# RWKV grams of a two-block transformer kernel: masked tiles of one kind each

## The chip, the cores and the metric

The kernel runs on one core of a Trainium2 chip. A core has a matrix engine (TensorE, PE in the profile; its weight loads are listed as PEld), three engines for elementwise work (VectorE or DVE, ScalarE or ACT, GpSimd or POOL), SyncE (SP), which here issues the weight transfers, and DMA queues. Each engine works through its own instructions in order and waits on semaphores for the others. The metric is the device time of one execution in microseconds (us), given as the median of several runs.

## The reference

The program takes 256 tokens of width 2048 in fp32 through two blocks. The first is a hybrid: one projection `u = rmsnorm(x) @ w_in` feeds an attention with forget gates ("fox", 8 heads of 128) and an RWKV7 recurrence (16 heads of 64), whose outputs are gated and merged. The second block joins a gated convolution, a latent attention and a memory attention. The change concerns the recurrence, which the reference writes step by step:

```python
def step(S, inp):
    r_t, w_t, k_t, v_t, kk_t, b_t = inp
    sa = jnp.einsum('bhvk,bhk->bhv', S, -kk_t)
    S = (S * w_t[:, :, None, :] + sa[..., None] * b_t[:, :, None, :]
         + v_t[..., None] * k_t[:, :, None, :])
    y = jnp.einsum('bhvk,bhk->bhv', S, r_t)
    return S, y
...
y = _rwkv7_scan(rh, heads(decay), kh, vh, kk, kk * ah)
mu = jnp.mean(y, axis=-1, keepdims=True)
var = jnp.mean(jnp.square(y - mu), axis=-1, keepdims=True)
y = ((y - mu) * lax.rsqrt(var + GN_EPS)).reshape(B, T, RWKV_WIDTH)
y = y * rwkv_ln_w.astype(f32) + rwkv_ln_b.astype(f32)
...
o_b = (y + bonus.reshape(B, T, RWKV_WIDTH)) * jax.nn.silu(z_b)
...
o_a = o_a.astype(x.dtype) @ w_proj_fox
o_b = o_b.astype(x.dtype) @ w_proj_rwkv
m = jax.nn.sigmoid(g_a) * o_a + jax.nn.sigmoid(g_b) * o_b
return x + m @ w_out
```

## The kernel before

**GEMMs.** All projections run as one stream of weight blocks of 512 KB. SyncE fetches a block into `raw` (L402), ScalarE rounds it to `whi` (helper at L278), VectorE takes `wlo = raw - whi` (helper at L241), and TensorE multiplies (L286) with activations split in the same way: three products (whi with the high part, whi with the low part, wlo with the high part), which together give fp32 precision. There are four `raw` and four `whi`/`wlo` buffers. A product is named by its GEMM: `acc.fq`, `acc.fk`, `acc.fv`, `acc.fz` (fox), `acc.zb` (the RWKV gate), `acc.ga` and `acc.gb` (the gates of the merge), `acc.pf` and `acc.pr` (the two output projections), and so on; `acc.gb` comes right after the last `acc.pf` column.

**Side work.** RWKV, fox heads and the like are generators ("jobs"). Between weight blocks a planner steps them: it keeps clocks of estimated costs for each engine and decides at each block which job goes one `yield` on. A scheduler then puts the resulting instructions in an order per engine and gives out the buffers. So the order of instructions on an engine depends on the costs of the steps and on when buffers come free. Two pools matter here: `a4` gives 32 slots of 128 x 1024 words in SBUF, and three PSUM banks serve the side work (grams, attention scores `fs`, transposes `fpt`, outputs `fo`), while five banks hold the GEMMs' sums. A tile that is handed out is sometimes claimed by a one-element memset on VectorE (L565): it stands in VectorE's order, and whoever writes the tile first waits for it.

**RWKV.** A job treats 8 heads, so it runs in two halves (about 115 to 375 us and 400 to 635 us). The 256 tokens are cut into four chunks `c` of 64, the heads into four pairs `j`; a unit `u = 4j + c` is one pair in one chunk, so there are 16. Per unit and head `hh` of the pair, TensorE forms the gram of `AR` and `BK`. Its left 64 columns (kind r = 0) are masked strictly and its right 64 columns (r = 1) inclusively by the constant `rmask` (128 columns). This is done in four rounds `q` of four units: eight matmuls into two PSUM banks (one per `hh`), a `yield`, two mask products on VectorE into the tile `GG`, four DMAs on GpSimd's queue that copy 32 x 32 corners of the strict part to DRAM (`Ld`, L954), a `yield`. The strict part is read three times: through `Ld` by the inversion of the triangular systems (tiles `W`, `LB`, `Xd`, `XA`), by the matmul `u` (L995 and around) and by `zl` (L1024). `zl` stands ahead of the loop over four chunks (L1031 on). The inclusive part is read in that loop by `yp` (L1073). Behind the loop come `CE` and `SQ` (centred outputs and squares), `head_rs` (mean squares `hs` by matmul, an inverse square root by integer steps and Newton steps on VectorE in the tiles `hms`, `ht`, `hg`, `hy`, then `hy` written to DRAM as `hd` and read back spread over partitions as `hr`, L622 to L627), then `CE *= hr`, `BV += CE`, `BV *= szb`, and the split of `BV` into `obh`, `obl`, which `acc.pr` multiplies.

**Fox.** For each head `fs` (scores) goes through softmax on VectorE and ScalarE (`sm`, `mx`), is transposed by TensorE (`fpt`, L1184), copied to `PT` on ScalarE and multiplied by the values (`fo`). These steps stand between the RWKV steps in zb, between 410 and 460 us.

**Merge.** `gate` is the sigmoid of `acc.ga` or `acc.gb` (ScalarE), `mf` is gate times `acc.pf` (VectorE). Both are `a4` tiles and are claimed.

Of the kernel before, what the change touches and what calls it, by code (L numbers as in the profile page):

```python
# [226 lines left out]
def hybrid_kernel(ctx: ExitStack, tc: tile.TileContext, io, out):  # L227
# [15 lines left out]
    def mul(o, a, b):  # L243
        tt(o, a, b, ALU.mult)
# [38 lines left out]
    def mm(o, l, r, start=True, stop=True):  # L283
        n = fsz(o)
        clock["pe"] += max(PEF + n / 2400.0, 0.109) if l.dtype == F32R else max(n / 600.0, fsz(l) / 1200.0)
        TE.matmul(o, lhsT=l, rhs=r, start=start, stop=stop)  # L286
# [17 lines left out]
    def a4(name, dt=F32):  # L304
        return apool.tile([128, 4, 256], dt, name=nm(name), tag="a4")
# [28 lines left out]
    def cc(n, p0=0, p1=128, c0=0, c1=None):  # L334
        o, w = CCOL[n]
        t, o = (con, o) if o < NCON2 else (con1, o - NCON2)
        return t[p0:p1, o + c0:o + (w if c1 is None else c1)]
# [391 lines left out]
    for b in range(4):  # L729
# [11 lines left out]
        for acc, cols, blocks in ((acc_l, 256, [b]), (acc_r, 512, [4 + 2 * b, 5 + 2 * b])):  # L741
            per = 1024 // cols
            for c, o in enumerate(acc):
                for e, j in enumerate(blocks):
                    for i in range(per):
                        k = per * e + i
                        w = slice(i * cols + 128 * c, i * cols + 128 * c + 128)
# [83 lines left out]
    def rwkv_job(b):  # L831
# [46 lines left out]
        for i in range(2):  # L878
            us = slice(8 * i, 8 * i + 8)
            for hh in range(2):  # L880
                p = slice(64 * hh, 64 * hh + 64)
# [8 lines left out]
        for i in range(2):  # L890
            us = slice(8 * i, 8 * i + 8)
            for hh in range(2):
                p = slice(64 * hh, 64 * hh + 64)
# [19 lines left out]
        SV = [a4("SV").rearrange("p a b -> p (a b)").rearrange("p (u k s) -> p u k s", u=8, k=2) for _ in range(2)]  # L913
        for i in range(2):
# [9 lines left out]
            ps3 = ps.rearrange("p (u s) -> p u s", u=8)  # L924
            for u in range(8):
                for hh in range(2):
                    p, q = slice(64 * hh, 64 * hh + 64), slice(64 - 64 * hh, 128 - 64 * hh)
# [4 lines left out]
            for hh in range(2):  # L932
                q = slice(64 - 64 * hh, 128 - 64 * hh)
                acopy(SV[i][q, :, hh, :], ps3[q, :, :])
            yield
        GG = []
        Ld = dpool.tile([2, 2, 16, 32, 32], F32, name=nm("Ld"), tag="Ld", bufs=2)
        for q in range(4):
            g = a4("GG").rearrange("p a b -> p (a b)").rearrange("p (u k r t) -> p u k r t", u=4, k=2, r=2)
            GG.append(g)  # L940
            pg = [bank("gram"), bank("gram")]
            for w in range(4):
                u = 4 * q + w
                for hh in range(2):
                    p = slice(64 * hh, 64 * hh + 64)
                    mm(pg[hh][:, 128 * w:128 * w + 128], BK[u // 8][p, u % 8, :, :], AR[u // 8][p, u % 8, :, :])
            yield
            for hh in range(2):
                mul(g[:, :, hh, :, :].rearrange("p u r t -> p u (r t)"), pg[hh].rearrange("p (u m) -> p u m", u=4),
                    cc("rmask").unsqueeze(1).to_broadcast([128, 4, 128]))  # L950
            for hh in range(2):
                for hf in range(2):
                    p0 = 64 * hh + 32 * hf
                    POOL.dma_start(out=Ld[hh, hf, 4 * q:4 * q + 4, :, :].rearrange("u s t -> s u t"),  # L954
                                   in_=g[p0:p0 + 32, :, hh, 0, 32 * hf:32 * hf + 32])
            yield
        W1, W2, W3 = a4("W1"), a4("W2"), a4("W3")
        LB = flat(W1)[0:64, :].rearrange("p (s t) -> p s t", s=32)
# [9 lines left out]
        for j in range(31):  # L968
            n, w = 31 - j, j + 1
# [11 lines left out]
        XA = b2("XA").rearrange("p (u c) -> p u c", u=16)  # L981
        for hh in range(2):
            POOL.dma_start(out=XA[64 * hh:64 * hh + 32, :, :], in_=Xd[hh, 0, :, :, :].rearrange("u t c -> t u c"))
            for hf in range(2):
                p0 = 64 * hh + 32 * hf
                POOL.dma_start(out=YF[p0:p0 + 32, :, 32 * hf:32 * hf + 32],
                               in_=Yd[hh, hf, :, :, :].rearrange("u s t -> s u t"))
# [4 lines left out]
        for u in range(16):  # L992
            for hh in range(2):
                p0 = 64 * hh
                mm(ps3[p0 + 32:p0 + 64, u, :], GG[u // 4][p0:p0 + 32, u % 4, hh, 0, 32:64], XA[p0:p0 + 32, u, :])  # L995
            if u == 7:
                yield
        yield
# [20 lines left out]
        for i in range(2):  # L1019
            zl = bank("zl").rearrange("p (u v) -> p u v", u=8)  # L1020
            for w in range(8):
                u = 8 * i + w
                for hh in range(2):
                    mm(zl[hs[hh], w, :], GG[u // 4][hs[1 - hh], u % 4, hh, 0, :], SV[i][hs[1 - hh], w, hh, :])  # L1024
                if w == 3:
                    yield
            yield
            acopy(ZL[:, 8 * i:8 * i + 8, :], zl)

        S = None  # L1030
        for c in range(4):  # L1031
            u_of = lambda j: 4 * j + c
            Z = ZL[:, c:16:4, :]
            yp = bank("yp")[:, :256].rearrange("p (j v) -> p j v", j=4)
            if S is not None:
                z = bank("z")[:, :256].rearrange("p (j v) -> p j v", j=4)
                for j in range(4):
                    u = u_of(j)
                    for hh in range(2):
                        mm(z[hs[hh], j, :], AR[u // 8][hs[hh], u % 8, 0, :], S[hs[hh], j, :])  # L1040

                for j in range(4):
                    u = u_of(j)
                    for hh in range(2):
                        mm(yp[hs[hh], j, :], S[hs[hh], j, :], AR[u // 8][hs[hh], u % 8, 1, :], start=j == 0, stop=False)
                yield
                add(Z, Z, z)
                yield
            sa = bank("sa")[:, :256].rearrange("p (j v) -> p j v", j=4)
            for j in range(4):  # L1050
                for hh in range(2):
                    mm(sa[hs[hh], j, :], YF[hs[hh], u_of(j), :], Z[hs[hh], j, :])
            yield
            for i in range(2):
                for hh in range(2):
                    o = SV[i][hs[hh], c:8:4, hh, :]
                    if hh:
                        vcopy(o, sa[hs[hh], 2 * i:2 * i + 2, :])
                    else:
                        acopy(o, sa[hs[hh], 2 * i:2 * i + 2, :])  # L1060
            yield
            S_old = S
            if c < 3:
                sp = bank("sp")[:, :256].rearrange("p (j v) -> p j v", j=4)
                for j in range(4):
                    u = u_of(j)
                    for hh in range(2):
                        mm(sp[hs[hh], j, :], BT[u // 8][:, u % 8, 64 * hh:64 * hh + 64], SV[u // 8][:, u % 8, hh, :])
            for j in range(4):
                u = u_of(j)  # L1070
                for hh in range(2):
                    mm(yp[hs[hh], j, :], SV[u // 8][:, u % 8, hh, :],
                       GG[u // 4][:, u % 4, hh, 1, :], start=S_old is None, stop=S_old is None or j == 3)  # L1073
            yield
            if c < 3:
                S = b1("S").rearrange("p (j v) -> p j v", j=4)
                pcb = pch.rearrange("p (j c) -> p j c", c=4)[:, :, c:c + 1].to_broadcast([128, 4, 64])
                if S_old is None:
                    mul(S, sp, pcb)
                else:  # L1080
                    add(S, sp, S_old)
                    mul(S, S, pcb)
            for i in range(2):
                acopy(AR[i][:, c:8:4, 1, :], yp[:, 2 * i:2 * i + 2, :])
            yield
# [190 lines left out]
    m, gb = [], []  # L1276
# [538 lines left out]
```

## Time and profile before

| | |
|---|---|
| median of 3 runs | 2041.01 us (2038.97 to 2042.87) |
| the profiled execution's own time | 2038.03 us |
| its span, first to last instruction | 2036.2 us |
| granted TensorE clock, mean | 0.996 |
| TensorE busy | 2008.4 us |
| VectorE busy | 1305.1 us |
| ScalarE busy | 976.9 us |
| GpSimd busy | 82.2 us |
| DMA, mean | 186 GB/s |

The times of one kernel's runs differ by up to 4 us; the profile comes from one execution. In the rows of the timeline stand start and duration in us, engine, line, operation, output and inputs by the names of the program, shape, and in brackets the idle time before the instruction with what ended it. PEclk is the granted clock of TensorE as a share of full speed. A row with "x4" joins neighbours of one kind.

### The profile page before, as it was taken

Reading aid. Unit: us, or ns where it says so; the run is one execution under the profiler, and the core shown is the slowest. Engines: PE = TensorE matmul, PEld = TensorE weight load, DVE = VectorE, ACT = ScalarE, POOL = GpSimd, SP = SyncE. Lnnn points to the kernel's source line nnn. Section 1 sums busy time; section 2 is a strip of 40 time slices with the busy share of each in tenths; the row PEclk is TensorE's granted clock in tenths of the full one; section 3 lists DMA queues with packets and bytes.
Section 4 is the critical chain, followed back from the end, with each engine's and each line's share of the span. In section 5 each row is a group of like instructions: output and inputs, shape, how many; then the busy total and the mean of one; then the engine's idle time right before and its main releaser. Section 6 shows DMA issues by size and latency. Waiting matters only on the chain. (4 is left out here: it accounts for less than half of the span.)

```text
span 2036.2 us, 31875 instructions
## 1 busy us (share of the span) xinstructions
PE 2008.4 (99%) x12702; PEld 1781.1 (87%) x12702; DVE 1305.1 (64%) x1989; ACT 976.9 (48%) x1330; POOL 82.2 (4%) x149
## 2 busy tenths in 40 slices
PE   9999999999998999999999999999999999999999
PEld 9999999888776888898999788889888889988887
DVE  8776847868446478665766676575765665555554
ACT  6734446344443455554555445445445444444432
POOL 0002000020000000000000100000000000000000
PEclk9999999999998999999999999999999999999999
DMA  7554644536545666565555665565664555566564
GB/s 271 163 187 155 196 130 141 177 114 197 172 157 196 215 208 200 197 214 189 187 189 172 200 202 167 176 230 168 197 215 160 193 176 168 195 214 209 191 202 145
DMA packets 106820, 378.52 MB, mean 186 GB/s; under 512 B 13178, under 2 KB 14162, under 8 KB 106672
## 3 DMA queue, kind: packets, MB, share of 16 engines
q1 hardware_dynamic: 97136, 350.11, 52.2%
q0 software_dynamic: 9104, 25.78, 4.4%
q8 instruction: 99, 1.62, 0.3%
q10 hardware_dynamic: 432, 0.61, 0.1%
q14 instruction: 49, 0.40, 0.1%
HBM read 367.32 MB, written 5.86 MB: 183 GB/s over the span
## 5 line engine op out<-in xcount | busy, mean ns | idle before, releaser
L241 DVE TENSOR_TENSOR wlo<-raw,whi 128x1024 fp32r<-128x1024 f32 (+1 forms) x659 | 801.7, 1222 | 556.2 <-ACT whi L278 550.1
L278 ACT ACTIVATE whi<-raw 128x1024 fp32r<-128x1024 f32 (+1 forms) x659 | 695.0, 1058 | 825.6 <-PE acc.lo L286 51.1
L286 PE MATMUL acc.lz<-h2l,whi 128*128 128x256 f32 x256 | 72.4, 284 | 0.0
L286 PE MATMUL acc.lz<-h2h,whi 128*128 128x256 f32 x256 | 72.3, 283 | 0.0
L286 PE MATMUL acc.lz<-h2h,wlo 128*128 128x256 f32 x256 | 72.0, 283 | 0.0
L286 PE MATMUL acc.gb<-wlo,hh 128*128 128x512 f32 x128 | 51.0, 398 | 8.2 <-DVE wlo L241 8.2
L286 PE MATMUL acc.gm<-wlo,h2h 128*128 128x512 f32 x128 | 50.0, 391 | 0.8 <-DVE wlo L241 0.8
L286 PE MATMUL acc.gb<-whi,hl 128*128 128x512 f32 x128 | 50.8, 397 | 0.0
L286 PE MATMUL acc.gb<-whi,hh 128*128 128x512 f32 x128 | 50.2, 397 | 0.4 <-ACT whi L278 0.4
L286 PE MATMUL acc.ga<-wlo,hh 128*128 128x512 f32 x128 | 50.6, 395 | 0.0
L286 PE MATMUL acc.ga<-whi,hl 128*128 128x512 f32 x128 | 50.3, 393 | 0.0
L286 PE MATMUL acc.gc<-wlo,h2h 128*128 128x512 f32 x128 | 50.1, 392 | 0.0
L286 PE MATMUL acc.gm<-whi,h2l 128*128 128x512 f32 x128 | 50.1, 392 | 0.0
L286 PE MATMUL acc.gl<-wlo,h2h 128*128 128x512 f32 x128 | 50.1, 391 | 0.0
L286 PE MATMUL acc.gc<-whi,h2l 128*128 128x512 f32 x128 | 50.1, 391 | 0.0
L286 PE MATMUL acc.gl<-whi,h2h 128*128 128x512 f32 x128 | 49.9, 391 | 0.0
L286 PE MATMUL acc.w<-wlo,mgh 128*128 128x512 f32 x128 | 49.9, 390 | 0.0
L286 PE MATMUL acc.wo<-wlo,mh 128*128 128x512 f32 x128 | 49.9, 390 | 0.0
L286 PE MATMUL acc.w<-whi,mgh 128*128 128x512 f32 x128 | 49.9, 390 | 0.0
L286 PE MATMUL acc.gc<-whi,h2h 128*128 128x512 f32 x128 | 49.9, 390 | 0.0
L286 PE MATMUL acc.wo<-whi,ml 128*128 128x512 f32 x128 | 49.8, 389 | 0.0
L286 PE MATMUL acc.gl<-whi,h2l 128*128 128x512 f32 x128 | 49.8, 389 | 0.0
(658 smaller groups left out, 5896.8 us busy)
## 6 DMA issues: line engine op xcount, KB each, us to landing
raw<-in_W SPq DMA_DIRECT2D x657, 512.0 KB, 3.8
hr<-hd POOLq DMA_DIRECT2D x10, 512.0 KB, 5.4
hr<-hd POOLq DMA_DIRECT2D x12, 256.0 KB, 4.2
xr<-in_xtm POOLq DMA_DIRECT2D x4, 512.0 KB, 6.1
mt<-in_memT POOLq DMA_DIRECT2D x4, 512.0 KB, 7.3
xbd<-x1g POOLq DMA_DIRECT2D x4, 512.0 KB, 4.1
xo<-xbd POOLq DMA_DIRECT2D x4, 512.0 KB, 4.8
out_tm<-xo SPq DMA_DIRECT2D x8, 256.0 KB, 4.7
```

Of the source, the lines that this page charges most:

```text
L241: DVE.tensor_tensor(out=o, in0=a, in1=b, op=op)
L278: ACT.activation(out=o, in_=a, func=f, scale=scale, **kw)
L286: TE.matmul(o, lhsT=l, rhs=r, start=start, stop=stop)
```

## The change

The four `GG` tiles of a half no longer hold one round each with both kinds, but one kind each: at q = 0 and q = 2 two tiles are taken together, the first for the strict parts of eight units, the second for the inclusive parts. Each mask product is cut in two by kind, so that sixteen products of 128 x (4 x 64) stand where eight of 128 x (4 x 128) stood. The readers index the new tiles; the DMAs keep count and size, and read with a stride of 128 words between units where it was 256. The number of tiles stays four per half; the last reader of two of them is now `zl`. Behind the change every line number is higher by 3.

```diff
         for q in range(4):
-            g = a4("GG").rearrange("p a b -> p (a b)").rearrange("p (u k r t) -> p u k r t", u=4, k=2, r=2)
-            GG.append(g)
+            if q % 2 == 0:
+                GG.append([a4("GG").rearrange("p a b -> p (a b)").rearrange("p (u k t) -> p u k t", u=8, k=2) for _ in range(2)])
+            g, gs = GG[q // 2], slice(4 * (q % 2), 4 * (q % 2) + 4)
             pg = [bank("gram"), bank("gram")]
...
-            for hh in range(2):
-                mul(g[:, :, hh, :, :].rearrange("p u r t -> p u (r t)"), pg[hh].rearrange("p (u m) -> p u m", u=4),
-                    cc("rmask").unsqueeze(1).to_broadcast([128, 4, 128]))
+
+            for r in range(2):
+                for hh in range(2):
+                    mul(g[r][:, gs, hh, :], pg[hh].rearrange("p (u r t) -> p u r t", u=4, r=2)[:, :, r, :],
+                        cc("rmask", 0, 128, 64 * r, 64 * r + 64).unsqueeze(1).to_broadcast([128, 4, 64]))
...
-                                   in_=g[p0:p0 + 32, :, hh, 0, 32 * hf:32 * hf + 32])
+                                   in_=g[0][p0:p0 + 32, gs, hh, 32 * hf:32 * hf + 32])
...
-                mm(ps3[p0 + 32:p0 + 64, u, :], GG[u // 4][p0:p0 + 32, u % 4, hh, 0, 32:64], XA[p0:p0 + 32, u, :])
+                mm(ps3[p0 + 32:p0 + 64, u, :], GG[u // 8][0][p0:p0 + 32, u % 8, hh, 32:64], XA[p0:p0 + 32, u, :])
...
-                    mm(zl[hs[hh], w, :], GG[u // 4][hs[1 - hh], u % 4, hh, 0, :], SV[i][hs[1 - hh], w, hh, :])
+                    mm(zl[hs[hh], w, :], GG[u // 8][0][hs[1 - hh], u % 8, hh, :], SV[i][hs[1 - hh], w, hh, :])
...
-                       GG[u // 4][:, u % 4, hh, 1, :], start=S_old is None, stop=S_old is None or j == 3)
+                       GG[u // 8][1][:, u % 8, hh, :], start=S_old is None, stop=S_old is None or j == 3)
```

The scheduler's order changes in three stretches: the first half of RWKV, zb, and the turn from pf to gb. First the turn to gb. VectorE's order before, from the last step of the second half's inverse square root (`hy`) on; blocks 982 to 1000 are gb's:

```order
L241 TENSOR_TENSOR hy_923_6496<-hy_923_6496,ht_924_6497 128x256
L565 MEMSET mf_934_6554 128x1
L261 SCALAR_TENSOR_TENSOR mf_934_6554<-gate_892_6342,acc.pf2_939_6563 128x512
L565 MEMSET gate_949_6636 128x1
L261 SCALAR_TENSOR_TENSOR mf_934_6554<-gate_892_6342,acc.pf2_938_6562 128x512
L565 MEMSET mf_976_6790 128x1
L565 MEMSET gate_991_6868 128x1
L241 TENSOR_TENSOR obl_998_6885<-BV_270_1935,obh_997_6884 128x1024
L261 SCALAR_TENSOR_TENSOR mf_976_6790<-gate_949_6636,acc.pf3_980_6798 128x512
L261 SCALAR_TENSOR_TENSOR CE_901_6386<-CE_901_6386,par_75,hr_930_6530 128x256 x4
L261 SCALAR_TENSOR_TENSOR BV_628_4519<-CE_901_6386,par_75,BV_628_4519 128x256 x2
L241 TENSOR_TENSOR wlo_983_6813<-raw_969_6738,whi_982_6812 128x1024
```

And of the change, from the second of gb's conversions on (the first, `wlo_983`, stands two rows further up, and the products of pf2 ahead of `hms`):

```order
L241 TENSOR_TENSOR wlo_986_6847<-raw_972_6772,whi_985_6846 128x1024
L261 SCALAR_TENSOR_TENSOR hy_929_6549<-hg_931_6551,hy_929_6549 128x256
L241 TENSOR_TENSOR wlo_989_6865<-raw_975_6790,whi_988_6864 128x1024
...
L241 TENSOR_TENSOR wlo_993_6887<-raw_979_6812,whi_992_6886 128x1024
L241 TENSOR_TENSOR hy_929_6549<-hy_929_6549,ht_930_6550 128x256
L565 MEMSET gate_949_6648 128x1
...
L241 TENSOR_TENSOR obl_998_6901<-BV_270_1935,obh_997_6900 128x1024
L261 SCALAR_TENSOR_TENSOR mf_976_6806<-gate_949_6648,acc.pf3_980_6814 128x512
L241 TENSOR_TENSOR wlo_1000_6913<-raw_984_6832,whi_999_6912 128x1024
L261 SCALAR_TENSOR_TENSOR CE_904_6426<-CE_904_6426,par_75,hr_939_6588 128x256 x4
L241 TENSOR_TENSOR wlo_1003_6933<-raw_987_6850,whi_1002_6932 128x1024
```

Four of gb's conversions moved from behind the product with `hr` to places between the steps of `hy`, a fifth to just ahead of it; the sixth stands right behind it. ScalarE's order at the same place, before:

```order
L278 ACTIVATE whi_977_6792<-raw_966_6720 128x1024
L278 ACTIVATE gate_949_6636<-acc.ga3_954_6645 128x512
L278 ACTIVATE obh_997_6884<-BV_270_1935 128x1024
L278 ACTIVATE gate_949_6636<-acc.ga3_953_6644 128x512
L278 ACTIVATE whi_982_6812<-raw_969_6738 128x1024
L278 ACTIVATE whi_985_6830<-raw_972_6756 128x1024
```

and of the change:

```order
L278 ACTIVATE whi_977_6808<-raw_966_6736 128x1024
L278 ACTIVATE whi_982_6828<-raw_969_6754 128x1024
L278 ACTIVATE whi_985_6846<-raw_972_6772 128x1024
L278 ACTIVATE whi_988_6864<-raw_975_6790 128x1024
L278 ACTIVATE whi_992_6886<-raw_979_6812 128x1024
L278 ACTIVATE gate_949_6648<-acc.ga3_954_6657 128x512
L278 ACTIVATE obh_997_6900<-BV_270_1935 128x1024
```

The evacuation of `acc.ga3` into `gate`, which waits for the claim on VectorE, moved behind four of gb's conversions. The second stretch is zb, on TensorE, from the last zb matmul ahead of a softmax transpose on; before:

```order
L286 MATMUL gram_692_4928<-AR_591_4310,BK_593_4312 128x128 x4
L286 MATMUL acc.zb1_742_5256<-hh_115_798,wlo_740_5251 128x256
L286 MATMUL gram_693_4929<-AR_591_4310,BK_593_4312 128x128 x4
L1184 MATMUL fpt_697_4965<-con_76,sm_686_4889 128x128 x3
L286 MATMUL fo_699_4983<-PT_698_4975,fv_581_4268 128x128 x3
L286 MATMUL gram_701_4988<-AR_591_4310,BK_593_4312 128x128
L286 MATMUL gram_702_4989<-AR_591_4310,BK_593_4312 128x128
...
L286 MATMUL fs_707_5033<-cneg_609,conr_83 128x256
L1184 MATMUL fpt_720_5111<-con_76,sm_712_5052 128x128 x3
L286 MATMUL fo_722_5141<-PT_721_5131,fv_581_4268 128x128 x3
```

and of the change, from the last of six zb matmuls between the first transpose and its `fo`:

```order
L286 MATMUL acc.zb1_745_5278<-hh_115_798,wlo_743_5273 128x256
L286 MATMUL fo_694_4954<-PT_693_4938,fv_581_4276 128x128 x3
L286 MATMUL gram_696_4969<-AR_596_4353,BK_598_4355 128x128 x4
L286 MATMUL gram_697_4970<-AR_596_4353,BK_598_4355 128x128 x4
...
L286 MATMUL fs_698_4985<-cneg_609,conr_83 128x256
L286 MATMUL gram_705_5021<-AR_597_4354,BK_599_4356 128x128 x4
L286 MATMUL gram_706_5022<-AR_597_4354,BK_599_4356 128x128 x4
L286 MATMUL gram_711_5083<-AR_597_4354,BK_599_4356 128x128 x4
L286 MATMUL gram_712_5084<-AR_597_4354,BK_599_4356 128x128 x4
L1187 MATMUL fpt_713_5099<-con_76,sm_702_5010 128x128 x3
L286 MATMUL fo_718_5131<-PT_717_5123,fv_581_4276 128x128 x3
```

One block of grams stood between the two `fo` (alternating between its two banks, in single rows), and now three do, each by four and four; the other grams of before stood among zb matmuls further up. VectorE's rows of the change between the scores `fs` of the second head and its transpose:

```order
L261 SCALAR_TENSOR_TENSOR sm_702_5010<-fs_698_4985,ctm_610,con1_77 128x256
L1153 TENSOR_REDUCE mx_707_5037<-sm_702_5010 128x1 x2
L241 TENSOR_TENSOR GG_703_5019<-gram_705_5021,con1_77 128x4x64
L241 TENSOR_TENSOR GG_704_5020<-gram_705_5021,con1_77 128x4x64
L241 TENSOR_TENSOR GG_703_5019<-gram_706_5022,con1_77 128x4x64
L241 TENSOR_TENSOR GG_704_5020<-gram_706_5022,con1_77 128x4x64
L1158 RECIPROCAL mx_707_5037<-mx_707_5037 128x2
L241 TENSOR_TENSOR GG_703_5019<-gram_711_5083,con1_77 128x4x64
L241 TENSOR_TENSOR GG_704_5020<-gram_711_5083,con1_77 128x4x64
L255 TENSOR_SCALAR sm_702_5010<-sm_702_5010,mx_707_5037 128x128
```

Six mask products stand there between the steps of the softmax, where before the steps followed one another. The third stretch is the first half's grams among the matmuls of fq on TensorE; the second block of grams before:

```order
L286 MATMUL acc.fq0_306_2163<-hh_104_725,wlo_290_2048 128x256
L286 MATMUL gram_316_2257<-AR_236_1651,BK_238_1653 128x128 x4
L286 MATMUL gram_317_2258<-AR_236_1651,BK_238_1653 128x128 x4
L286 MATMUL acc.fq0_303_2160<-hh_115_798,whi_294_2103 128x256
...
L286 MATMUL acc.fq0_304_2161<-hh_115_798,wlo_301_2155 128x256
L286 MATMUL gram_328_2339<-AR_237_1652,BK_239_1654 128x128 x4
```

and of the change:

```order
L286 MATMUL acc.fq0_303_2160<-hh_115_798,wlo_295_2104 128x256
L286 MATMUL gram_319_2271<-AR_236_1651,BK_238_1653 128x128
L286 MATMUL gram_320_2272<-AR_236_1651,BK_238_1653 128x128
...
L286 MATMUL acc.fq0_304_2161<-hh_115_798,whi_294_2103 128x256
...
L286 MATMUL gram_331_2369<-AR_237_1652,BK_239_1654 128x128
L286 MATMUL gram_332_2370<-AR_237_1652,BK_239_1654 128x128
```

Before, the first and third block alternated between the two banks row by row, and the second and fourth came by four and four; now all four alternate, with 24 fq matmuls between blocks instead of 18.

## The prediction

> **What bounds the kernel now.** I read the page's busy shares first, then the waits of TensorE, then the windows around its longest two, and last the rows of every engine there.
>
> ```profile
> span 2036.2 us, 31875 instructions
> PE 2008.4 (99%) x12702; PEld 1781.1 (87%) x12702; DVE 1305.1 (64%) x1989; ACT 976.9 (48%) x1330; POOL 82.2 (4%) x149
> ```
>
> TensorE is busy 99% of the span. Only 2036.2 − 2008.4 = 27.8 us are idle, so a reordering can win those, the time at a lowered clock, and what small matmuls waste; nothing else.
>
> ```profile
> PE acc.gb L286 <- DVE wlo L241: 8.2, 1, 8.2
> PE fpt L1184 <- DVE sm L255: 3.3, 1, 3.3
> ...
> PE u L286 <- DMA XA<-Xd: 0.8, 1, 0.8
> ```
>
> (waits of TensorE: total, times, longest.) The longest two lie in stretches where the change reorders work. In the windows the first figures are length, then busy time of PE, PEld, DVE, ACT, POOL (instructions in brackets), then the granted clock:
>
> ```profile
> 439.00:453.00 14.00, 10.08 (x67) 9.49 (x67) 10.21 (x32) 7.71 (x21) 4.67 (x8) 0.88 0.12 25
> 427.00:439.00 12.00, 11.42 (x96) 10.02 (x94) 7.45 (x17) 3.33 (x8) 6.52 (x12) 1.00 0.25 66
> 620.00:640.00 20.00, 11.41 (x38) 8.60 (x37) 14.83 (x33) 6.60 (x7) 3.49 (x6) 0.74 0.54 180
> 640.00:660.00 20.00, 20.00 (x89) 16.55 (x89) 8.58 (x7) 9.21 (x10) 0.00 (x0) 1.00 0.76 269
> ```
>
> From 620 to 640 us TensorE idles 20 − 11.41 = 8.59 us; from 427 to 453 us it idles (12 − 11.42) + (14 − 10.08) = 4.5 us.
>
> **Part 1: the stall at the start of gb.** Rows of ScalarE, VectorE, GpSimd and TensorE (start, duration, idle before and what ended it), and one window:
>
> ```profile
> 619.15 0.60 ACT L278 ACTIVATE gate<-acc.ga 128x512 f32<-128x512 f32 x1 [8.20 <-DVE gate L565]
> 619.65 3.88 ACT L278 ACTIVATE whi<-raw 128x1024 fp32r<-128x1024 f32 x4
> ...
> 618.06 0.43 DVE L241 TENSOR_TENSOR hy<-hy,ht 128x256 f32<-128x256 f32 x1
> 626.01 1.67 DVE L261 SCALAR_TENSOR_TENSOR CE<-CE,par,hr 128x256 f32<-128x256 f32 x4 [4.56 <-DMA hr<-hd]
> 628.40 1.22 DVE L241 TENSOR_TENSOR wlo<-raw,whi 128x1024 fp32r<-128x1024 f32 x1
> ...
> 620.98 1.28 POOL L627 DMA_DIRECT2D hr<-hd  x2 [1.65 <-PE acc.pf L286]
> ...
> 620.75 0.73 PE L286 MATMUL acc.gb<-whi,hh 128*128 128x512 f32 x2 [0.41 <-ACT whi L278]
> 629.67 0.79 PE L286 MATMUL acc.gb<-wlo,hh 128*128 128x512 f32 x1 [8.19 <-DVE wlo L241]
> 634.95 0.46 PE L286 MATMUL acc.gb<-wlo,hh 128*128 128x512 f32 x1
> ...
> 632.00:634.00 2.00, 2.00 (x6) 1.61 (x5) 2.00 (x4) 0.00 (x0) 0.00 (x0) 0.50 0.80 293
> ```
>
> ScalarE stood 8.20 us at a gate tile whose slot was claimed only behind hy; four conversions were queued behind it. VectorE then waited for hr ahead of gb's first wlo. TensorE, out of weights, idled, and restarted at clock 0.50: between 629.67 and 634.95 it started 12 matmuls in 5.28 us, where the pitch is 20/89 = 0.225 us, so 2.6 us more went. The stall costs 8.6 + 2.6 = 11.2 us.
>
> Before, the claims waited for the GG tiles, which the last chunk's yp reads. With the strict pair free after zl, CE and ycl take those slots, and the pf2 product takes YF's. The instruction order shows what follows: the four whi stand ahead of the gate evacuation, and their wlo between the steps of hy. The matmuls of gb need those four wlo at about 620.4, 621.8, 623.1 and 624.5 us (pitch 0.225 from the 620.2 at which gb begins). The four whi buffers come free as pf3 leaves its blocks, 24, 18, 12 and 0 matmuls ahead of gb (614.8, 616.1, 617.5 and 620.2 us). With one whi (3.88 / 4 = 0.97), one wlo (1.22) and the steps of hy between them, the wlo end at about 617.3, 618.9, 620.6 and 623.0: each over 1 us early.
>
> What is late next is hr. The chain to hy now has four conversions (4 × 1.22 us) between its steps and ends at about 623.5 instead of 618.5. Before, hr landed 626.0 − 618.5 = 7.5 us behind hy. The first half's read-back, with weights streaming beside it, gives the same:
>
> ```profile
> 373.68 0.41 DVE L241 TENSOR_TENSOR hy<-hy,ht 128x256 f32<-128x256 f32 x1
> 381.42 1.23 DVE L241 TENSOR_TENSOR KK<-KK,hr 128x1024 f32<-128x1024 f32 x1 [5.57 <-DMA hr<-hd]
> ```
>
> 381.42 − 374.09 = 7.3 us. So hr lands at about 631.0, CE (1.67) and the wlo behind it (1.22) end at about 634.0, and gb's sixth block needs it 62 matmuls after its start minus the 48 for four blocks and 12 for the fifth, that is at 620.2 + 62 × 0.225 = 634.1. The slack is nearly nothing; I allow 0.4 us. Part 1: **−10.8**.
>
> **Part 2: softmax and grams in zb.**
>
> ```profile
> 432.42 1.16 PE L286 MATMUL gram<-AR,BK 64*128 64x128 f32 x8
> 434.91 0.55 PE L1184 MATMUL fpt<-con,sm 128*128 128x128 f32 x3
> 436.03 0.94 PE L286 MATMUL fo<-PT,fv 128*128 128x128 f32 x6 [0.58 <-ACT PT L278]
> 436.90 1.16 PE L286 MATMUL gram<-AR,BK 64*128 64x128 f32 x16
> 442.48 0.61 PE L1184 MATMUL fpt<-con,sm 128*128 128x128 f32 x3 [3.34 <-DVE sm L255]
> 443.67 1.45 PE L286 MATMUL fo<-PT,fv 128*128 128x128 f32 x6 [0.58 <-ACT PT L278]
> ...
> 438.67 1.28 DVE L241 TENSOR_TENSOR GG<-gram,con 128x512 f32<-128x512 f32 x2
> 439.87 0.73 DVE L261 SCALAR_TENSOR_TENSOR sm<-fs,ctm,con 128x128 f32<-128x128 f32 x2
> 441.85 0.17 DVE L1155 RECIPROCAL mx<-mx 128x2 f32<-128x2 f32 x1 [0.73 <-ACT sm L278]
> ...
> 445.00:447.00 2.00, 2.00 (x9) 1.82 (x9) 1.43 (x4) 1.84 (x6) 1.14 (x3) 0.50 0.45 115
> ```
>
> Idle here is 0.58 + 3.34 + 0.58 = 4.5 us. The price of a narrow mask product (VectorE) is bracketed by two rows, the old one and the nearest of half its width that also reads PSUM:
>
> ```profile
> L241 DVE TENSOR_TENSOR GG<-gram,con x16: 680/684/692, 179.9 to 439.3; 128x512 f32<-128x512 f32 x16
> L257 DVE TENSOR_SCALAR hms<-hs x16: 417/420/425, 115.4 to 1608.4; 128x256 f32<-128x256 f32 x16
> ```
>
> I take 0.42 us by width; the upper end is 0.684. Sixteen instead of eight per half make 6.7 instead of 5.5 us, at most 10.9; VectorE has 36% of the span free, so only the place matters. In the new order two matmul groups go elsewhere: six zb matmuls fill the wait ahead of the first fo (−0.58), and two blocks of grams (16 rows) now lie between the two fo, in the hole of 3.34 us. Replayed with the rows above from the first fo: grams to 2.5, fs to 3.45, four mask products and sm to 4.7, mx to 5.3, four products to 7.0, reciprocal, two products to 8.0, sm·mx to 8.5, fpt 8.4, fo 9.5. TensorE is idle some 2.3 us in it, in pieces under 1.5. Idle falls from 4.5 to about 2.3, so **−2.2**; with products at 0.684 ten of them add 2.6 and the gain is gone. The third softmax had 120 zb matmuls as cover and now has 62:
>
> ```profile
> 445.84 0.99 PE L286 MATMUL fs<-cneg,conr 128*128 128x128 f32 x2
> 449.46 0.28 PE L286 MATMUL acc.zb<-hh,wlo 128*128 128x256 f32 x1
> 449.58 0.28 PE L286 MATMUL acc.zb<-hh,whi 128*128 128x256 f32 x1
> ...
> 453.61 0.53 DVE L255 TENSOR_SCALAR sm<-sm,mx 128x128 f32<-128x128 f32 x2
> ```
>
> 62 × 0.12 = 7.4 us stand against the 454.1 − 446.8 = 7.3 that its sm·mx took from fs, so 0 to 1.5 us of idle may come up there. The range of the part is −4 (the clock's dip goes too) to +2.
>
> A rule bears on the dip. The row: clock 0.50 between 445 and 447, behind a wait of 3.34 us. The Trainium skill, "TensorE: Matmul & The Clock Gate", Part 1, says that the gate falls to half after one idle window of about 3.4 us and opens after about 3.4 us of work. The rows of gb agree (0.50 after 8.19 us, full again some 5 us into the work). By that rule pieces under 1.5 us leave the clock full, and the sum would be about 1.5 us lower; I leave the dip in.
>
> **Part 3: grams and visits.** A block of grams costs TensorE by its order:
>
> ```profile
> 178.44 1.16 PE L286 MATMUL gram<-AR,BK 64*128 64x128 f32 x16
> 181.88 1.71 PE L286 MATMUL gram<-AR,BK 64*128 64x128 f32 x16
> ```
>
> Alternating between the two banks a block takes 1.16 us, by four and four 1.71. In the first half four alternating blocks replace two of each: −1.1. In zb three blocks by four and four (1.71 each) and one alternating replace two of 1.16, two groups of 1.16 each, and one split 3-3-1-1: +0.2. TensorE changes two times more between GEMM and small work; at about 0.2 us each (the gap to a neighbour's pitch on both sides), +0.4. Part 3: **−0.5**, −1.5 to +1.5, since TensorE is 100% busy in the first half and a wait there would show at once.
>
> The second half's u (0.8 us behind XA) moves by two matmuls with its chain: 0, ±1. The 16 Ld transfers per half are as many and as large. From gb's second column on TensorE's order is the old one and it is the bound, so what is won stays won.
>
> **Sum.** The profiled execution took 2038.0 us for its span of 2036.2. 2038.0 − 10.8 − 2.2 − 0.5 = 2024.5. The median of the runs, 2041.0, stands 3.0 above that execution, so 2027.5, say **2028**.
>
> **The rivals.** (a) *The wait for hr remains.* CE still stands in VectorE's queue ahead of gb's sixth wlo and all behind it; each us that hr is late costs one. Against it: 7.3 and 7.5 us measured. For it: the slack is 0.1, and hr's landing alone varies:
>
> ```profile
> DMA to landing us min/median/max: 3.7/5.2/6.6
> ```
>
> (all hr transfers.) hd took 2.2 us here (618.8 to 621.0) and hr 5.0; both at 6.6 would be 6 us more, and past some 3 us the clock falls too (2.6). Less the 0.4 already allowed, late by 2 gives 2029, by 4 2034, by 6 2036.
>
> (b) *Little reaches the end.* The stretch at gb turns out to be held by something else that ends as late (the bank of ga3, whose evacuation still waits for the claim behind hy, needed at about 625.6), or parts 2 and 3 eat it. With part 1 gone 2027.5 + 10.8 = 2038; with part 2 at its upper end 2042.5.
>
> (c) *Slower.* hy itself comes late: its steps now queue behind conversions that wait for a free whi buffer, and so for TensorE; TensorE then waits for VectorE's hr. PE runs dry at 634.1; the old stall is back when hr lands 8.6 us later than reckoned, at 639.6. With part 2 at its upper end (+4.2 against the sum) the time passes 2045 from 11.2 us later, 642.2. That is hy at 629.0 and both transfers at their slowest at once. 2046.
>
> **How the numbers follow.** Forecast 0.59 (2023 to 2033 by parts 2 and 3); (a) 0.19; (b) 0.14; (c) 0.08. A measurement of this kernel tells 0.2% (4.1 us) from no change: faster means under 2036.9. The forecast and nearly all of (a) lie there: 0.76; (b) and the rest of (a) within it: 0.16; (c) slower: 0.08. Range 2022.5 to 2039.5: from parts 2 and 3 and the median's spread at their good ends, to (b) without the upper end of part 2; above lie (c) and half of (b).
>
> **What would show it.** Right: no wait of acc.gb above 1 us, 88 or more matmuls from 620 to 640, clock 1.00 there; fo to fo about 9.5 us with no wait over 2; narrow products near 0.42; gram blocks of 1.16 in fq. Wrong: acc.gb waiting for wlo at about 634, with CE released by hr just before, is (a); waiting at 625 for a bank is (b); fpt waiting over 3.5 us unsays part 2.

## The result and the profile after

The change takes 2023.64 us (median of 4 runs, 2022.89 to 2025.07) against 2039.99 us before (4 runs, 2037.16 to 2042.87): ratio 0.9922, 95% interval 0.991 to 0.9934, so 16.35 us less. The profiled execution took 2022.89 us. Its page and the longest waits of TensorE (total, times, longest) with those that the prediction named:

```profile
span 2021.0 us, 31907 instructions
PE 2004.6 (99%) x12702; PEld 1778.0 (88%) x12702; DVE 1305.3 (65%) x2005; ACT 977.3 (48%) x1330; POOL 82.1 (4%) x149
```

```profile
PE acc.vr L286 <- DVE wlo L241: 2.5, 1, 2.5
...
PE fo L286 <- ACT PT L278: 0.6, 1, 0.6
PE acc.gb L286 <- DVE wlo L241: 0.6, 1, 0.6
PE fpt L1187 <- DVE sm L255: 0.5, 1, 0.5
```

The two long waits, 8.2 us at `acc.gb` and 3.3 us at `fpt`, are 0.6 and 0.5 us now; the wait of `u` is no longer among those of 0.2 us and more. TensorE runs the same 12702 matmuls in 3.8 us less busy time, mostly by its clock; VectorE has 16 instructions more and is as busy as before.

Where in the program the time went is read from the first start of a GEMM's matmuls in the views by tile (duration min/median/max in ns, then first and last start). Before and after:

```profile
L286 PE MATMUL acc.zb<-hh,whi x128: 277/283/435, 390.5 to 467.7; 128*128 128x256 f32 x128
L286 PE MATMUL acc.ga<-whi,hh x128: 387/389/398, 468.1 to 607.6; 128*128 128x512 f32 x128
L286 PE MATMUL acc.pr<-whi,obh x64: 389/389/477, 718.9 to 764.6; 128*128 128x512 f32 x64
```

```profile
L286 PE MATMUL acc.zb<-hh,whi x128: 278/283/385, 391.8 to 464.4; 128*128 128x256 f32 x128
L286 PE MATMUL acc.ga<-whi,hh x128: 388/389/502, 464.7 to 603.5; 128*128 128x512 f32 x128
L286 PE MATMUL acc.pr<-whi,obh x64: 388/389/478, 704.0 to 749.6; 128*128 128x512 f32 x64
```

From zb to ga is 468.1 − 390.5 = 77.6 us before and 72.9 after (−4.7); from ga to pr, which holds the turn to gb, 250.8 and 239.3 (−11.5). The same view gives 30.8 and 29.7 for the stretch fq to fk (−1.1), 186.5 and 187.5 from fk to zb (+1.0), 953.2 and 952.8 from pr to `acc.lz` in the second block. The profiled execution of the change reached fq 1.4 us later, ahead of any changed instruction. The spans differ by 1.4 − 1.1 + 1.0 − 4.7 − 11.5 − 0.4 + 0.1 = −15.2 us.

**The turn to gb.** Rows of VectorE, ScalarE, GpSimd and TensorE after, and the window that stood at 11.41 us busy before:

```profile
611.91 1.23 DVE L241 TENSOR_TENSOR wlo<-raw,whi 128x1024 fp32r<-128x1024 f32 x1 [0.16 <-ACT whi L278]
...
613.39 1.22 DVE L241 TENSOR_TENSOR wlo<-raw,whi 128x1024 fp32r<-128x1024 f32 x1
...
614.86 1.22 DVE L241 TENSOR_TENSOR wlo<-raw,whi 128x1024 fp32r<-128x1024 f32 x1
...
617.36 1.23 DVE L241 TENSOR_TENSOR wlo<-raw,whi 128x1024 fp32r<-128x1024 f32 x1 [0.16 <-ACT whi L278]
618.50 0.42 DVE L241 TENSOR_TENSOR hy<-hy,ht 128x256 f32<-128x256 f32 x1
...
627.98 1.67 DVE L261 SCALAR_TENSOR_TENSOR CE<-CE,par,hr 128x256 f32<-128x256 f32 x4 [2.55 <-DMA hr<-hd]
629.57 1.22 DVE L241 TENSOR_TENSOR wlo<-raw,whi 128x1024 fp32r<-128x1024 f32 x1
...
616.27 1.06 ACT L278 ACTIVATE whi<-raw 128x1024 fp32r<-128x1024 f32 x1 [1.66 <-PE acc.pf L286]
...
618.98 0.60 ACT L278 ACTIVATE gate<-acc.ga 128x512 f32<-128x512 f32 x1 [0.22 <-DVE gate L565]
...
622.75 1.28 POOL L627 DMA_DIRECT2D hr<-hd  x2 [2.98 <-DMA hd<-hy]
...
616.07 0.39 PE L286 MATMUL acc.gb<-whi,hh 128*128 128x512 f32 x1
...
620.00:640.00 20.00, 19.44 (x86) 15.80 (x85) 14.31 (x33) 8.68 (x9) 3.18 (x6) 1.00 0.67 219
```

Of gb's first four conversions two end before gb begins at 616.07, the third at 616.08, and the fourth ends at 618.59, just as the last step of `hy` starts. ScalarE reaches the gate tile behind the four `whi` and stands 0.22 us at its claim, where it stood 8.20 before. CE still waits for `hr`, and the conversion behind CE ends at 630.79: that is what is left of the wait, 0.56 us. 86 matmuls start between 620 and 640 us instead of 38 (the prediction's sign was 88 or more), at clock 1.00 instead of 0.74.

**zb.** Rows of TensorE, the window over the whole stretch after, and the group of narrow mask products (ns min/median/max); that window before was 45.50 us busy at clock 0.97:

```profile
432.64 0.94 PE L286 MATMUL fo<-PT,fv 128*128 128x128 f32 x6
433.50 1.71 PE L286 MATMUL gram<-AR,BK 64*128 64x128 f32 x16
...
436.22 3.33 PE L286 MATMUL gram<-AR,BK 64*128 64x128 f32 x32
440.07 0.55 PE L1187 MATMUL fpt<-con,sm 128*128 128x128 f32 x3 [0.51 <-DVE sm L255]
441.20 0.94 PE L286 MATMUL fo<-PT,fv 128*128 128x128 f32 x6 [0.58 <-ACT PT L278]
...
410.00:460.00 50.00, 48.44 (x450) 46.23 (x449) 35.94 (x87) 26.45 (x52) 11.20 (x20) 1.00 0.44 138
...
L241 DVE TENSOR_TENSOR GG<-gram,con x32: 408/417/425, 181.4 to 440.4; 128x256 f32<-128x256 f32 x32
```

The grams now fill the hole in which the second `fo` waited for its softmax: `fo` to `fo` takes 441.20 − 432.64 = 8.56 us, idle time over the 50 us falls from 4.5 to 1.56, and the clock stays at 1.00.

### The profile page after: what moved, and what is told of

Same layout as the page of the kernel before. It is cut to its first block, busy times and chain, and to the rows that moved or that the text cites. A ratio compares the mean times of both kernels' runs of the same rounds, so it can differ in the third digit from the quotient of the medians.

```text
span 2021.0 us, 31907 instructions
## 1 busy us (share of the span) xinstructions
PE 2004.6 (99%) x12702; PEld 1778.0 (88%) x12702; DVE 1305.3 (65%) x2005; ACT 977.3 (48%) x1330; POOL 82.1 (4%) x149
## 5 line engine op out<-in xcount | busy, mean ns | idle before, releaser
L286 PE MATMUL acc.ga<-whi,hh 128*128 128x512 f32 x128 | 50.0, 392 | 0.0
L286 PE MATMUL acc.w<-whi,mgl 128*128 128x512 f32 x128 | 49.8, 389 | 0.0
```

## The experiments

The theory on record (call it **slots**) was that the gain comes from letting the strict tiles go ahead of the chunk loop: other tiles take those slots earlier, and claims that waited no longer do. The rival (**charge**) came from reading the planner. Every elementwise helper adds a cost to a clock that decides when a job takes its next step:

```python
clock["dve"] += CD + fsz(o) / 960.0                       # L240, in the helper that mul calls; CD = 0.15 us
...
if clock[e] > before[e]:
    self.ready = max(self.ready, clock[e] + HOP)          # L434, Job.step
...
return self.done or (not self.soft and clock["pe"] < self.ready)
```

Sixteen products instead of eight carry eight more times `CD`, 1.2 us per half, whatever tile they write. RWKV's steps then become ready later in the stream of weight blocks, and the whole order after them may come out another way. All ratios below are against the kernel before. The table gives stretches (us) of each run's profile, read as above, with the wait of `acc.gb` for `wlo`. In charge_0_9 and ahead some side work moves ahead of zb, so fk to ga is the fairer stretch there: 256.2 and 255.5, against 264.1 before and 260.4 in the change.

| kernel | ratio, 95% interval | zb to ga | ga to pr | pr to lz | gb's wait |
|---|---|---|---|---|---|
| before | 1 | 77.6 | 250.8 | 953.2 | 8.2 |
| the change | 0.9922, 0.991 to 0.9934 | 72.9 | 239.3 | 952.8 | 0.6 |
| split_only | 0.9924, 0.9908 to 0.9941 | 73.0 | 239.9 | 953.3 | 1.2 |
| hold | 0.993, 0.9916 to 0.9945 | 73.8 | 239.7 | 953.4 | 0.7 |
| charge16 | 0.9957, 0.9942 to 0.9972 | 73.7 | 240.9 | 959.9 | 1.8 |
| charge8 | 1.0005, 0.9996 to 1.0015 | 78.7 | 249.2 | 953.9 | 8.4 |
| late_gb | 0.9968, 0.9956 to 0.998 | 77.6 | 238.8 | 956.1 | 0.2 |
| zb_only | 0.9966, 0.9955 to 0.9978 | 72.8 | 249.4 | 953.5 | 8.0 |
| charge_0_9 | 0.9921, 0.9904 to 0.9937 | 65.6 | 245.5 | 954.5 | 4.9 |
| ahead | 0.9902, 0.9889 to 0.9916 | 65.3 | 239.4 | 954.5 | 0.5 |
| change_again | 0.9918, 0.9904 to 0.9931 | 73.8 | 240.1 | 952.9 | 1.5 |

### split_only: the old tiles, the products cut in two

```diff
-            for hh in range(2):
-                mul(g[:, :, hh, :, :].rearrange("p u r t -> p u (r t)"), pg[hh]...,
-                    cc("rmask")...)
+            for r in range(2):
+                for hh in range(2):
+                    mul(g[:, :, hh, r, :], pg[hh]...[:, :, r, :],
+                        cc("rmask", 0, 128, 64 * r, 64 * r + 64)...)
```

> The old four tiles with both kinds, each product cut in two by kind as in the change (16 narrow products per half), so no strict part is let go ahead of the loop. Theory S (freed slots, the prediction's): the stall at gb comes back, acc.gb waits about 8 us for wlo and the clock falls to 0.50; only what zb and the fq grams gave is kept: about 2034 to 2036. Theory P (the planner charges VectorE's clock for eight more products per half, and that alone moves the order of everything behind): the order at gb is the changed one and the time is the change's, 2023.6 within 1.

Measured 2024.6 us, the time of the change within the intervals, with the change's order of instructions on every engine. ScalarE's row at the gate tile is that of the change:

```profile
619.87 0.60 ACT L278 ACTIVATE gate<-acc.ga 128x512 f32<-128x512 f32 x1 [0.22 <-DVE gate L565]
```

Here each tile still holds both kinds, so none is let go ahead of the loop. Releasing the strict parts is not needed for the gain.

### hold: the change, with the strict tiles kept to the end of the loop

```diff
+            if c == 3:
+                for g in GG:
+                    DVE.tensor_copy(g[0][0:1, 0, 0, 0:1], AR[0][0:1, 3, 1, 0:1])
```

> The change, with one element of each strict tile written behind the last chunk's evacuation (two VectorE copies of one element per half, which the planner isn't charged for), so that the strict slots come free only behind the loop. Theory S: the stall at gb returns, 2033 to 2036. Theory P: as the change, 2023.6, within 1.

One element of each strict tile is written in the last chunk, when nothing reads the tile any more. Measured 2026.43 us. That is 1.8 us above what Charge (Theory P of the expectations) allowed, but its interval, 0.9916 to 0.9945, overlaps the change's, 0.991 to 0.9934, and it is far from the 2033 to 2036 of Slots (Theory S). gb's wait is 0.7 us, so the order there is the new one. Slots falls a second time.

### charge16: the kernel before, charged like the change

```diff
+            clock["dve"] += 2 * CD
```

stands behind the mask products of each round, so that the eight wide products are charged like sixteen.

> The kernel before, instruction for instruction the same work with wide products and old tiles; only the planner's VectorE clock is charged two more fixed costs per round of grams, as if the products were sixteen. Theory S: nothing moves that frees a slot, the stall at gb stays: 2040 less at most 5 for zb. Theory P: most or all of the gain, 2023 to 2026.

Measured 2032.18 us, between what the two theories forecast. The tiles and the instructions are those of before, and yet both stretches improve as in the change: `acc.pr` begins at 705.6 us, 13.3 us earlier than before and 1.6 later than in the change. Half of that is lost again in the second block, whose order comes out differently in a few rows; there TensorE waits longer than in the change, whose wait at `acc.gm` is 1.1 us and which has none at `ls`:

```profile
PE acc.gm L286 <- DVE wlo L241: 3.7, 1, 3.7
...
PE ls L286 <- DVE kn L261: 1.9, 1, 1.9
```

So the charge alone gives the gain of the RWKV stretches, and the rest of the program answers to the same charge with a loss of 959.9 − 953.2 = 6.7 us.

### charge8: the change, charged like before

```diff
+            clock["dve"] -= 2 * CD
```

> The change, tiles and narrow products as they are; only the planner's VectorE clock is charged two fixed costs less per round of grams, as if the products were eight. Theory S: slots are free ahead of the loop, the stall at gb is gone: 2026 to 2030. Theory P: the old order with its stalls at gb and in zb, 2039 to 2042 (8 more short products per half on VectorE, beside other work).

Measured 2041.37 us: nothing is left of the gain. Its tiles are those of the change, and its strict slots do go to `CE` and `ycl`, as the prediction had it (the slot of `YF` goes to `hr`, not to the pf2 product); but ScalarE stands at the gate tile as before, and both waits are back:

```profile
PE acc.gb L286 <- DVE wlo L241: 8.4, 1, 8.4
PE fpt L1188 <- DVE sm L255: 3.5, 1, 3.5
```

```profile
622.79 0.60 ACT L278 ACTIVATE gate<-acc.ga 128x512 f32<-128x512 f32 x1 [8.20 <-DVE gate L565]
```

The strict slots are free and nothing is won. Old and new tiles, wide and narrow products have now each run under the old and the new charge, and the turns at gb and in zb go with the charge: it is the cause of the gain. The run prices the products too: sixteen narrow ones with before's waits around them cost no more than the interval, 1.0005 (0.9996 to 1.0015).

### late_gb and zb_only: one stretch each

```diff
+        if b == 1:
+            clock["dve"] += 4.8
         yield from head_rs(SQ, 0, 1.0 / 64.0, 64e-5)
```

is late_gb: before's kernel, with a charge ahead of the second half's inverse square root alone. A charge of 3.6 there leaves before's order as it is, 4.8 turns it. And zb_only charges each round of mask products 0.2 instead of charge16's 0.3 (0.05 leaves before's order as it is, 0.1 does not):

```diff
+            clock["dve"] += 0.2
```

> The kernel before with no other edit than 4.8 us more on the planner's VectorE clock ahead of the second half's head_rs (instructions and tiles as before). TensorE's order is the old one through zb, ga and pf; at the turn to gb it is the changed one, and in the second block some rows differ. If the turn to gb is worth what the prediction's part 1 says whatever the slots do: acc.pr begins about 10.5 us earlier than before, fpt still waits 3.3 us in zb. The end by how the second block falls: 2030 if it is as before, 2036 to 2038 if it loses the 7 us that charge16 lost there. Theory S: no gain at gb, since no slot is freed.

> The kernel before with 0.2 us more per round of grams on the planner's VectorE clock (instructions and tiles as before). The order is the changed one in the fq grams and in zb, and the old one at gb and behind. If the parts add up: the wait of acc.gb for wlo stays at 8.2 us, ga begins 3 to 5 us earlier than before, and the whole is 2035 to 2037.

Measured 2032.47 and 2032.05 us: late_gb lies between its two forecasts, since its second block loses less than 7 us, and zb_only comes out 3 us better than forecast. The waits of late_gb, then those of zb_only:

```profile
PE acc.gm L286 <- DVE wlo L241: 3.6, 1, 3.6
PE fpt L1186 <- DVE sm L255: 3.3, 1, 3.3
...
PE acc.gb L286 <- DVE wlo L241: 0.2, 1, 0.2
```

```profile
PE acc.gb L286 <- DVE wlo L241: 8.0, 1, 8.0
...
PE fpt L1185 <- DVE sm L255: 0.4, 1, 0.4
```

The first has the old zb and the new gb (ga to pr −12.0, less 2.9 lost from pr to lz), the second the new zb and the old gb (zb −4.8, ga to pr −1.4). zb_only's 1.4 us lie in ga and pf, where it has the change's order too: its wait of `acc.gb` is 0.2 us shorter than before's, and the wait of `u` (0.8) is gone. The two stretches are separate gains, each set by its own turn of the order, and they add up to within 2 us: −12.0 − 4.8 − 1.4 = −18.2 against the change's −11.5 − 4.7 = −16.2.

### charge_0_9: more of the same charge

```diff
+            clock["dve"] += 0.9
```

> The kernel before with 0.9 us more per round of grams on the planner's VectorE clock (instructions and tiles as before). In zb every block of grams and every transpose now stands among zb matmuls; at gb the conversions stand between the steps of hy as in the change, but two of them ahead of its first step, and gb's fifth wlo too stands behind the product with hr. If only waits count: no wait in zb (1 us better than the change there), and at gb a wait for hr of 2 to 5 us, one for one with its landing: 2024 to 2030. If that wait is hidden, 2022.

Measured 2023.21 us: no better than the change in sum, but not the same program. zb has no wait of TensorE left, and gb shows the wait of the prediction's rival (a), though not for its reason, a late `hr`: the fifth conversion now stands behind CE too, so gb needs `hr` one block earlier, and everything waits for it. A window of zb, and rows of gb:

```profile
410.00:460.00 50.00, 50.00 (x460) 47.70 (x460) 33.44 (x68) 26.13 (x48) 11.20 (x20) 1.00 0.50 160
...
623.61 1.67 DVE L261 SCALAR_TENSOR_TENSOR CE<-CE,par,hr 128x256 f32<-128x256 f32 x4 [4.99 <-DMA hr<-hd]
...
625.60 1.22 DVE L241 TENSOR_TENSOR wlo<-raw,whi 128x1024 fp32r<-128x1024 f32 x1
```

```profile
PE acc.gb L286 <- DVE wlo L241: 4.9, 1, 4.9
```

`hr` was back 7.3 us behind `hy`, sooner than in the change. What costs 4.9 us is one place in VectorE's order.

### ahead and change_again: zb without a wait, and CE late

ahead has both charges, 0.9 in each round and 4.8 ahead of the second half's `head_rs`; change_again is the change once more, on the same chip.

> The kernel before (instructions and tiles as before) with 0.9 us more per round of grams and 4.8 us more ahead of the second half's head_rs on the planner's VectorE clock. Order: zb as in charge_0_9 (no wait), and at gb nine conversions ahead of the product with hr instead of five or four. If hr is the only thing that waits at gb, acc.gb has no wait above 0.5 us although hr lands as late, and acc.pr begins at 699 to 701. The second block has the order that cost 3 (late_gb) to 7 us (charge16) more: 2020 to 2026 at the end. If something else bounds gb (a bank, the claims), it waits there all the same.

> The change as it is, on the chip of the run beside it, for a comparison on one chip: 2022 to 2026 at a ratio of 0.991 to 0.993; its zb may or may not show the clock at 0.50 around 441 us, since of two kernels with one order (the change and hold) one did and one did not.

Measured 2019.6 us for ahead and 2023.05 for the change; the intervals of the two ratios (0.9889 to 0.9916, 0.9904 to 0.9931) overlap, but every run of ahead (2018.72 to 2021.82) lies below every run of the change (2022.38 to 2024.14). ahead keeps before's tiles and instructions. Nine conversions of gb stand ahead of CE:

```profile
620.05 0.42 DVE L241 TENSOR_TENSOR hy<-hy,ht 128x256 f32<-128x256 f32 x1
...
626.75 1.22 DVE L241 TENSOR_TENSOR wlo<-raw,whi 128x1024 fp32r<-128x1024 f32 x1 [0.36 <-ACT whi L278]
633.15 1.67 DVE L261 SCALAR_TENSOR_TENSOR CE<-CE,par,hr 128x256 f32<-128x256 f32 x4 [5.18 <-DMA hr<-hd]
```

`hr` came back 633.15 − 620.47 = 12.7 us behind `hy`, the slowest of all runs, and `acc.gb` waited only 0.5 us for it.

## Why the prediction came out as it did

**The time.** Forecast 2028, measured 2023.64, inside the range and faster, as forecast. Against the span the sum was 13.5 us; 15.2 came. The profiled execution after lies only 0.75 us below its median, where 3.0 were added; that part of the miss is the spread of the runs.

**Part 1, the size: right.** −10.8 forecast, −11.5 from ga to pr. Worked out from waits and clock it is the same: gb's waits 8.6 to 0.6 make 8.0, the lowered clock 2.6, and `u`, put at 0 ± 1, gave its 0.8. The replay held: the four conversions were to end 2.9 and 1.3 us ahead of gb's start and 0.4 and 2.8 behind it; they ended 2.9 and 1.5 ahead, at 0.0, and 2.5 behind. `hy` was to end 3.3 us into gb and ended 2.9 into it.

**Part 1, the reason: wrong.** The step that failed stands in these sentences: "Before, the claims waited for the GG tiles, which the last chunk's yp reads. With the strict pair free after zl, CE and ycl take those slots, and the pf2 product takes YF's." The slots go as it says, but they do not set the order: charge8 has the strict slots and gains nothing, split_only lacks the release and gains all, hold takes it away and keeps gb. Rows of before say the same, the last `yp` that reads a GG tile (start 596.6 us) and the gate's claim:

```profile
L286 PE MATMUL yp<-GG,SV x128: 222/222/270, 272.9 to 596.6; 128*64 128x64 f32 x128
...
619.05 0.06 DVE L565 MEMSET gate<- 128x1 f32 x1
```

The claim came 22 us after the tile was free. It did not wait for the tile but stood behind `hy` in VectorE's order. In place of the slots stands the planner's charge: eight fixed costs more per half, on paper 1.2 us, make RWKV's steps ready some blocks later, `head_rs` falls among gb's conversions instead of ahead of them, and the gate tile whose claim stands behind `hy` no longer stands ahead of the four `whi` on ScalarE. late_gb moves that one step alone and gets 12.0 us. The new order was known before the run, so the time came out of it rightly whatever had caused it; the reason itself explained nothing, and freeing more slots in the hope of more would have rested on a cause that these runs speak against here.

**The slack of `hr`: mis-sized.** 7.3 and 7.5 us were taken; the change had 9.06, hold 8.89, split_only 9.74, change_again 9.99, charge16 10.34. gb's waits largely follow: 0.56, 0.72, 1.24, 1.5 and 1.85 us, 1.3 us more wait for 1.3 us more delay from the change to charge16. With 0.4 allowed this cost 0.2 to 1.4 us, and the sign "no wait of acc.gb above 1 us" holds in the profiled run but not in change_again. So rival (a) was real and small.

Where the 7.5 us came from explains most of it. Windows from the issue of `hd` to the issue of `hr`, before and after (the last two figures are the DMA engines' busy share and GB/s):

```profile
618.78:620.98 2.20, 1.79 (x8) 1.17 (x8) 2.20 (x7) 1.83 (x3) 0.56 (x1) 1.00 0.02 4
...
619.21:622.75 3.54, 3.54 (x17) 2.92 (x16) 2.07 (x3) 0.37 (x1) 0.56 (x1) 1.00 0.51 174
```

Before, the write of `hd` had the DMA engines nearly to itself: ScalarE had just stood 8.20 us at the gate and converted no block, and the weight stream stood still (4 GB/s). The change removes that stand, the weights flow, and the same write takes 3.5 us instead of 2.2. The first half's 7.3 us, taken as a check "with weights streaming beside it", were measured at a share of 0.20 only. The profiled executions of all eleven rows of the table sort this way: 2.2 to 2.3 us at a share up to 0.04, 3.4 to 4.8 at 0.43 and more. No run varies the load alone, so that the load is the cause is argued.

**Part 2: the mechanism right, the size too small.** −2.2 forecast, −4.7 from zb to ga (−3.8 in change_again and hold). The narrow product took 0.417 us where 0.42 was taken, and the rounds of grams do lie between the two `fo`. The replay gave 9.5 us from `fo` to `fo` and 2.3 us of idle; it took 8.56, and 1.56 us are idle in the whole stretch, so 2.9 us of idle went instead of 2.2. Most of the rest is the clock: before's mean of 0.97 over 50 us is 1.5 us, which was left in. So the profiled run passes the part's own bound of −4. "I leave the dip in" is what failed here, in the profiled run; in others (hold, charge16, change_again) the dip is there.

**Part 3: right, and too fine to see whole.** Four alternating blocks of grams in the first half were to give −1.1; they take 1.16 us each, and fq to fk is 1.1 us shorter (1.0 in zb_only). The +0.6 for packing and visits disappears in ±1 us by which fk to zb differs between runs (186.5 before, 187.5 after, 188.1 in charge8).

**Rivals (b) and (c)** did not come: no bank held gb, and `hy` ended at 618.9, not at 629.

**What stays open.** Why the second block turns its order in charge16 and late_gb and not in the change was not followed beyond the waits at `acc.gm` and `ls`. Nor was it followed step by step how 1.2 us of charge per half grow into a turn at gb for which a single charge of 3.6 us there is not enough. That free slots help elsewhere, where the planner's costs stay fixed, is not excluded; a kernel with more `a4` slots was not run.

## What to carry to other kernels

Where a planner lays out the program from estimated costs, an edit acts twice: by what its instructions do, and by what they are charged. Run the edit with the old charge and the old code with the new charge before believing any reason for its time. And when a charge of a fraction of a microsecond can turn an order worth 12 us, look for the few places where a late result stands in a queue ahead of work that TensorE needs, and put that order there on purpose: ahead, with before's own instructions, came out 3.5 us under the change by the medians. And a time that is read beside a stall belongs to the stall: the read-back that the change had to hide became longer when the stall went.

## What the runs showed of the hardware

**The clock can dip without a long wait.** TensorE's same order in zb ran at full clock in the profiled executions of the change, split_only and zb_only, and for some 3 us at half clock in those of change_again, hold and charge16, behind waits of at most 0.58 us. hold's rows and its window (length, busy PE, PEld, DVE, ACT, POOL, then clock), then the change's window:

```profile
438.82 0.55 PE L1190 MATMUL fpt<-con,sm 128*128 128x128 f32 x3 [0.52 <-DVE sm L255]
439.95 1.65 PE L286 MATMUL fo<-PT,fv 128*128 128x128 f32 x6 [0.58 <-ACT PT L278]
...
440.00:442.00 2.00, 2.00 (x9) 2.00 (x10) 0.00 (x0) 0.37 (x2) 1.33 (x3) 0.50 0.16 31
```

```profile
440.00:442.00 2.00, 1.35 (x10) 1.15 (x11) 0.79 (x3) 0.49 (x1) 2.00 (x4) 1.00 0.14 27
```

Six `fo` matmuls took 1.65 us in the one and 0.94 in the other; from zb to ga the three with the dip took 73.7 to 73.8 us, the three without 72.8 to 73.0. The Trainium skill, "TensorE: Matmul & The Clock Gate", Part 1, ties the fall to one idle window of about 3.4 us, counted by a window that runs freely. The long waits agree (half clock after 8.19 us); these rows do not, since no idle piece here reaches 0.6 us. Ahead of them lie 7 us of grams, scores and transposes (432.25 to 439.37 in hold) with no zb matmul among them, in all six; whether such work counts as idle, and what decides between the executions, no run here tells.

**A read-back through DRAM has no fixed time.** `hy` to CE, one write of 8 KB (`hd`) and two reads of 256 KB (`hr`) on one queue, took from 7.3 us (charge_0_9) to 12.7 us (ahead) at the same place in the program. The write took 2.2 to 2.3 us at a DMA share of 0.04 or less and 3.4 to 4.8 at 0.43 to 0.70; the rest, from the issue of `hr` to CE, took 4.8 to 5.3 us in every run but ahead (8.2), which stays unexplained. An order that leaves such a result no slack is right in one run and late in the next; ahead's, with four more conversions in front of CE than the change's, took 12.7 us with a wait of 0.5 us.
